# Multi-query attention: pacing value products and waiting VectorE work by ScalarE's clock

## The chip, the cores and the metric

The kernel runs on one core of a Trainium2 chip. A core has five engines that run side by side, each through its own list of instructions in a fixed order: TensorE (PE in the profile, its weight loads PEld) multiplies matrices, ScalarE (ACT) evaluates the exponential, VectorE (DVE) does elementwise work, GpSimd (POOL) and SyncE (SP) here mostly issue DMAs. The metric is device time in microseconds. The kernel before takes 1087.03 us, the median of six runs that lie between 1085.57 and 1087.64 us.

## The reference

```python
def setup_inputs():
    batch, seq_len, embed_dim = (8, 1024, 1024)
    num_heads = 16
    head_dim = embed_dim // num_heads
    # q: (8, 1024, 16, 64); k, v: (8, 1024, 64), float32

def reference(q, k, v):
    q = q.transpose(0, 2, 1, 3)
    k = k[:, None, :, :].copy()
    v = v[:, None, :, :].copy()
    scores = np.matmul(q, k.transpose(0, 1, 3, 2)) / np.sqrt(head_dim)
    weights = np.exp(scores - np.max(scores, axis=-1, keepdims=True))
    weights = weights / np.sum(weights, axis=-1, keepdims=True)
    attn_out = np.matmul(weights, v)
    return attn_out.transpose(0, 2, 1, 3).astype(np.float32)
```

Sixteen query heads of a batch share one key and one value head. The kernel leaves out the maximum, sums the exponentials with a matrix product by ones, and divides at the end.

## The kernel before, in words

The work is cut into 64 pairs (8 batches of 8 head pairs), and a pair `p` into 8 key tiles `j` of 128 keys. For a key tile TensorE makes two score tiles (`unit`, L134; tile `sc`, 128 x 2 x 512, three buffers in PSUM), one for each half of the queries. A score tile becomes weights in one of two ways. For most key tiles ScalarE takes the exponential (L147) straight into `wt`. For 71 of the 512 key tiles (9 of every 64, `is_dve`) VectorE makes it (`exp_dve`): two instructions `z` that take the two score tiles out of PSUM (L158, issued at once), and then six more, `f`, `t`, `g` (L170 to L174), `t`, `g` and `wt` (L176 to L178), which go on a list `late` and are issued when the planner finds room. Score tiles of such a key tile are woven with those of the next one, so ScalarE has its own tiles meanwhile.

The value products follow. `av_slot` makes slot `i` of a pair's 24: eight slots with ones (group 0, L193, the sums), eight for each half of the queries with the values (groups 1 and 2, L201). In each group the VectorE-made tile comes last. A group adds up in one accumulator `acc`, out of two PSUM buffers (`b1p`), and VectorE copies it to `ots` (L208). After group 2 a DMA transpose turns the result (`turn`), and `finish` puts the reciprocal (L223) and the normalising product (L230, then the output DMA) on `late`.

The order of the instructions is written out when the program is built (`manual_schedule`), by a loop over 512 cycles `cy`, one for each key tile: two score tiles, then value slots up to a quota, then waiting VectorE work. Three things set it. The quota is three slots a cycle, 12 cycles behind the scores (`LAG`). The list `late` is served while VectorE's planned time `busy` is below `(cy + 1) * T_CYCLE`, with planned costs per instruction (`T_TS`, `T_TT`, ...). And `av_slot` calls `force`, which issues whatever is left of a tile's six instructions just ahead of the first product that reads it. When the chip runs, each engine goes through its list in that order and waits where an operand or a buffer isn't ready; the planner's times play no part then. The pool of weight tiles has `LAG + 8` buffers.

Of the kernel before, what the change touches and what calls it, by code (L numbers as in the profile page):

```python
# [22 lines left out]
LAG = 12  # L23
T_CYCLE = 1.53
# [4 lines left out]
def kernel(  # L29
# [45 lines left out]
    otq: dict = {}  # L75
    late: list = []
# [22 lines left out]
    def trans_k(b):  # L99
        st = kst[b]  # L100
        kps = b1p.tile([P, S], FP16, tag="b1", name=f"kps{b}")
# [80 lines left out]
    def av_slot(p, i):  # L182
# [3 lines left out]
        if n == 0:  # L186
            acc[p] = b1p.tile([P, QC], FP32, tag="b1", name=f"acc{p}_{grp}")
# [17 lines left out]
        if n == NKT - 1:  # L205
            if grp == 0:
                ots[p] = otsp.tile([P, 3, QC], FP16, tag="ots", name=f"ots{p}")
            vec(T_COPY, lambda: nc.vector.tensor_copy(out=ots[p][:, grp, :], in_=a))  # L208

    def turn(p):  # L210
        otq[p] = otqp.tile([P, 13, P], FP16, tag="otq", name=f"otq{p}")[:, 0:12, :]
        nc.sync.dma_start_transpose(
            out=otq[p], in_=ots[p].rearrange("p g x -> p (g x)")
        )

    def finish(p, cycle):
        b, hp = divmod(p, HP)
        o = otq[p]
# [3 lines left out]
        def reciprocal():  # L222
            nc.vector.reciprocal(  # L223
# [5 lines left out]
        def normalise():  # L229
            nc.vector.tensor_tensor(  # L230
# [13 lines left out]
        late.append((None, cycle, T_NORM, normalise))  # L244

# [20 lines left out]
    slots = [(p, i) for p in range(NP) for i in range(3 * NKT)]  # L266

# [4 lines left out]
    with tc.manual_schedule(engines={ENG.PE, ENG.Activation, ENG.DVE}):  # L272
# [4 lines left out]
        cy = 0  # L277
        while cy < NCY or done < len(slots) or late:
            w, c = divmod(cy, NKT)
# [5 lines left out]
            busy[0] = max(busy[0], cy * T_CYCLE)  # L285
            if cy < NCY:
                for t, h in units[2 * cy : 2 * cy + 2]:
                    unit(t // NKT, NQC * (t % NKT) + h)
            quota = 3 * (cy + 1 - LAG) + max(0, cy + 1 - (NCY - 2 * NKT))
            if cy >= NCY:  # L290
                quota = len(slots)
            while done < min(quota, len(slots)):
                p, i = slots[done]
                if NKT * p + NKT - 1 >= cy and i % NKT + NKT * p >= cy:
# [3 lines left out]
                if i == 3 * NKT - 1:  # L298
                    turn(p)
                    finish(p, cy + 6)  # L300
            nb = w // HP + 1
            if nb < B and w % HP == HP - 2:
                if c == 2:
                    cast_k(nb)
                if c == 7:
                    trans_k(nb)
            while True:
                e = next((e for e in late if cy >= e[1] or done == len(slots)), None)
# [35 lines left out]
```

## Time and profile before

| | |
|---|---|
| median of six runs | 1087.03 us (1085.57 to 1087.64) |
| the profiled execution | 1086.96 us, of which the span from first to last instruction is 1085.2 us |
| TensorE's mean granted clock | 0.909 of full speed |
| PE busy | 813.0 us, 75% of the span |
| ACT busy | 825.7 us, 76% |
| DVE busy | 780.3 us, 72% |
| DMA | 89 GB/s over the span |

The rows are of one profiled execution. A busy time counts overlap of neighbouring instructions on an engine, so one activation of 1.02 us may stand 0.9 us after the one before. "Idle before" is the time in which an engine had nothing to do ahead of an instruction, with the instruction that ended it. No engine is busy throughout, and the chain of waits that ended last is spread over three of them: ACT 33%, DVE 29%, PE 28%.

### The profile page before, as it was taken

The numbers are of one execution on the slowest core, as the hardware profiler recorded it, in microseconds if no ns is written. First come the engines' busy times: TensorE is split into PE (matmuls) and PEld (weight loads), VectorE is DVE, ScalarE is ACT, GpSimd is POOL, SyncE is SP. The second block draws the span as 40 slices with busy tenths as digits, with TensorE's granted clock in tenths as the row PEclk, the third lists the DMA queues.
The fourth block names the chain that finished last, engine by engine and source line by source line (L and its number), as shares of the span: only waits on it lengthen the run. The fifth ranks groups of instructions, "written<-read, shape, count | busy, mean of one in ns | idle before, by whom it ended". The sixth has DMA issues, their size and how long they took to land.

```text
span 1085.2 us, 15328 instructions
## 1 busy us (share of the span) xinstructions
PE 813.0 (75%) x6208; PEld 234.6 (22%) x6208; DVE 780.3 (72%) x914; ACT 825.7 (76%) x883; POOL 64.1 (6%) x78
## 2 busy tenths in 40 slices
PE   3887778857788577876778777787777877788775
PEld 1222222212222122221222212222222222122121
DVE  1788677965779757796678956689567885678863
ACT  4998688956789477995779858797577976778763
POOL 3000000000000000000000000000000000000000
PEclk9999898987999789997899979899789998899888
DMA  9365465643656445573455635465354654434324
GB/s 135 54 108 107 73 103 88 108 82 66 101 88 104 87 73 95 85 127 66 76 96 91 114 73 90 76 100 105 63 98 71 108 95 73 88 64 88 78 49 107
DMA packets 317766, 96.41 MB, mean 89 GB/s; under 512 B 252160, under 2 KB 317696, under 8 KB 317696
## 3 DMA queue, kind: packets, MB, share of 16 engines
q1 hardware_dynamic: 242816, 77.62, 33.7%
q0 software_dynamic: 74880, 17.83, 17.6%
q8 instruction: 48, 0.79, 0.3%
q14 instruction: 22, 0.18, 0.1%
HBM read 37.75 MB, written 33.55 MB: 66 GB/s over the span
## 4 chain that ended last, share of the span: by engine, by line
ACT 33%; DVE 29%; PE 28%; issue 7%; DMA 2%; ACTq 0%; POOL 0%; DVEq 0%; POOLq 0%
DMA qt_126<-qn_104 1%; DMA qn_104<-in_q_dram 1%; PE acc_1_2671 L201 0%; DMA otq_10800<-ots_10762 0%; PE acc_1_6347 L201 0%; PE acc_1_6855 L201 0%; PE acc_1_8031 L201 0%; PE acc_1_4507 L201 0%; PE acc_1_9371 L201 0%; PE acc_1_2835 L201 0%; PE acc_1_5847 L201 0%; PE acc_1_9535 L201 0%; PE acc_1_1659 L201 0%; PE acc_1_9863 L201 0%; PE acc_1_3167 L201 0%
## 5 line engine op out<-in xcount | busy, mean ns | idle before, releaser
L193 PEld LDWEIGHTS <-ones_98 128*32 128x32 f16 x2048 | 42.5, 95 | 239.3 <-issue 224.6
L134 PEld LDWEIGHTS <-k2t_124 64*128 64x128 f16 x256 | 12.3, 97 | 65.7 <-issue 64.5
L134 PEld LDWEIGHTS <-k2t_1183 64*128 64x128 f16 x256 | 11.5, 95 | 49.1 <-issue 48.9
L134 PEld LDWEIGHTS <-k2t_6543 64*128 64x128 f16 x256 | 11.4, 95 | 48.8 <-issue 48.6
L134 PEld LDWEIGHTS <-k2t_2523 64*128 64x128 f16 x256 | 11.3, 95 | 49.3 <-issue 49.1
L134 PEld LDWEIGHTS <-k2t_7883 64*128 64x128 f16 x256 | 11.3, 95 | 48.5 <-issue 48.3
L134 PEld LDWEIGHTS <-k2t_3863 64*128 64x128 f16 x256 | 11.3, 95 | 48.7 <-issue 48.4
L134 PEld LDWEIGHTS <-k2t_5203 64*128 64x128 f16 x256 | 11.2, 96 | 48.3 <-issue 48.2
L134 PEld LDWEIGHTS <-k2t_9223 64*128 64x128 f16 x256 | 11.0, 95 | 46.4 <-issue 46.2
L201 PEld LDWEIGHTS <-v_351 128*64 128x64 f16 x256 | 12.1, 118 | 24.9 <-issue 21.8
L201 PEld LDWEIGHTS <-v_4363 128*64 128x64 f16 x256 | 12.1, 118 | 24.6 <-issue 21.4
L201 PEld LDWEIGHTS <-v_8383 128*64 128x64 f16 x256 | 12.3, 114 | 21.4 <-issue 16.1
L201 PEld LDWEIGHTS <-v_5703 128*64 128x64 f16 x256 | 11.9, 116 | 22.9 <-issue 19.5
L201 PEld LDWEIGHTS <-v_1683 128*64 128x64 f16 x256 | 11.8, 115 | 23.2 <-issue 19.7
L201 PEld LDWEIGHTS <-v_3023 128*64 128x64 f16 x256 | 11.8, 115 | 23.1 <-issue 19.7
L201 PEld LDWEIGHTS <-v_7043 128*64 128x64 f16 x256 | 11.8, 115 | 22.7 <-issue 19.4
L201 PEld LDWEIGHTS <-v_102 128*64 128x64 f16 x256 | 11.4, 112 | 20.2 <-issue 16.4
L158 DVE TENSOR_SCALAR z_4_174<-sc_8_170 128x1024 uint16<-128x1024 f32 x1 | 1.2, 1223 | 16.3 <-PE sc_8_170 L134 16.3
L147 ACT ACTIVATE wt_0_137<-sc_0_134 128x1024 f16<-128x1024 f32 x1 | 1.0, 1023 | 15.2 <-PE sc_0_134 L134 15.2
L134 PE MATMUL sc_0_134<-qt_126,k2t_124 64*128 64x512 f16 x2 | 0.6, 593 | 10.0 <-DMA qt_126<-qn_104 10.0
L147 ACT ACTIVATE wt_7_6522<-sc_14_6519 128x1024 f16<-128x1024 f32 x1 | 1.0, 1023 | 7.0 <-PE sc_14_6519 L134 7.0
L147 ACT ACTIVATE wt_7_5182<-sc_14_5179 128x1024 f16<-128x1024 f32 x1 | 1.0, 1023 | 7.0 <-PE sc_14_5179 L134 7.0
(4438 smaller groups left out, 2908.0 us busy)
## 6 DMA issues: line engine op xcount, KB each, us to landing
out_dram<-osb_423 SPq DMA_DIRECT2D x1, 512.0 KB, 3.9
out_dram<-osb_584 SPq DMA_DIRECT2D x1, 512.0 KB, 3.8
out_dram<-osb_751 SPq DMA_DIRECT2D x1, 512.0 KB, 4.8
out_dram<-osb_915 SPq DMA_DIRECT2D x1, 512.0 KB, 4.8
out_dram<-osb_1084 SPq DMA_DIRECT2D x1, 512.0 KB, 3.2
out_dram<-osb_1260 SPq DMA_DIRECT2D x1, 512.0 KB, 4.8
out_dram<-osb_1424 SPq DMA_DIRECT2D x1, 512.0 KB, 3.8
out_dram<-osb_1590 SPq DMA_DIRECT2D x1, 512.0 KB, 3.8
```

The source lines that it names most:

```text
L134: nc.tensor.matmul(sc[:, h, :], k2t[64 * h : 64 * h + 64, j * P : (j + 1) * P], qt[p].rearrange("p c x -> p (c x)")[64 * h : 64 * h + 64, ...
L147: nc.scalar.activation(out=wt[p, j][:, :, c * QC : (c + 1) * QC], in_=sc, func=EXP, scale=ascale)
L158: vec(2 * T_COPY, lambda: nc.vector.tensor_scalar(out=z[:, :, c * QC : (c + 1) * QC], in0=sc, scalar1=15 * ONE, scalar2=None, op0=ALU.add,))
L193: nc.tensor.matmul(a[32 * g : 32 * g + 32, :], ones16, w[:, h, cq * QC : (cq + 1) * QC], start=(n == 0), stop=(n == NKT - 1), tile_positio ...
L201: nc.tensor.matmul(a[64 * h : 64 * h + 64, :], vt[:, j, :], w[:, h, cq * QC : (cq + 1) * QC], start=(n == 0), stop=(n == NKT - 1), tile_po ...
```

## The change

Every instruction of the kernel before is there after it, and no other; each engine has as many rows as before. What changes is the order:

- The planner's time is now `clock`, which grows by `T_ACT` = 0.905 us for each score tile that ScalarE takes and by nothing for VectorE's; before it was 1.53 us for every cycle.
- The quota of value slots follows that clock: 24 slots in `t_pair`, the clock's advance over a mean pair, and `LAG` = 14 key tiles behind. Towards the end the quota is also raised by 4.5 slots a cycle. The pool of weight tiles grows from 20 to 22 buffers.
- Within a cycle waiting VectorE work now comes ahead of the value slots, and behind the score tiles.
- The copy of an accumulator is no longer issued at once: it goes on a list `first` for the next cycle, served ahead of `late`; `release` issues it at the latest when another tile of the two-buffer pool is taken. The DMA transpose follows the copy of group 2, and `finish` is due five cycles after that copy.
- The planner now also counts the two VectorE jobs of a new batch's keys.

```diff
--- before.py
+++ after.py
@@ -20,8 +20,8 @@
 GB = 0.07826797
 
 DVE_TILES = 9
-LAG = 12
-T_CYCLE = 1.53
+LAG = 14
+T_ACT = 0.905
 T_COPY, T_REC, T_NORM, T_TS, T_TT = 0.6, 0.2, 1.13, 0.6, 1.13
 
 
@@ -73,6 +73,8 @@
     acc: dict = {}
     ots: dict = {}
     otq: dict = {}
+    cy = [0]
+    first: list = []
     late: list = []
     busy = [0.0]
 
@@ -98,6 +100,7 @@
 
     def trans_k(b):
         st = kst[b]
+        release()
         kps = b1p.tile([P, S], FP16, tag="b1", name=f"kps{b}")
         for c in range(NKT):
             nc.tensor.transpose(
@@ -184,6 +187,7 @@
         j = sorted(range(NKT), key=lambda j: (is_dve(NKT * p + j), j))[n]
         force((p, j))
         if n == 0:
+            release()
             acc[p] = b1p.tile([P, QC], FP32, tag="b1", name=f"acc{p}_{grp}")
         a = acc[p]
         w = wt[p, j]
@@ -205,9 +209,16 @@
         if n == NKT - 1:
             if grp == 0:
                 ots[p] = otsp.tile([P, 3, QC], FP16, tag="ots", name=f"ots{p}")
-            vec(T_COPY, lambda: nc.vector.tensor_copy(out=ots[p][:, grp, :], in_=a))
+
+            def evacuate():
+                nc.vector.tensor_copy(out=ots[p][:, grp, :], in_=a)
+                if grp == 2:
+                    turn(p)
+
+            first.append((None, cy[0] + 1, T_COPY, evacuate))
 
     def turn(p):
+        finish(p, cy[0] + 5)
         otq[p] = otqp.tile([P, 13, P], FP16, tag="otq", name=f"otq{p}")[:, 0:12, :]
         nc.sync.dma_start_transpose(
             out=otq[p], in_=ots[p].rearrange("p g x -> p (g x)")
@@ -215,11 +226,11 @@
 
     def finish(p, cycle):
         b, hp = divmod(p, HP)
-        o = otq[p]
         osb = osbp.tile([P, NKT, 2 * D], FP32, tag="osb", name=f"osb{p}")
         rec = recp.tile([P, NQC, 4, 2], FP32, tag="rec", name=f"rec{p}")
 
         def reciprocal():
+            o = otq[p]
             nc.vector.reciprocal(
                 out=rec,
                 in_=o[:, 0:4, :].rearrange(
@@ -227,6 +238,7 @@
             )
 
         def normalise():
+            o = otq[p]
             nc.vector.tensor_tensor(
                 out=osb.rearrange("p i (h d) -> p (i h) d", h=2),
                 in0=o[:, 4:12, :].rearrange("p i (h d) -> p (i h) d", h=2),
@@ -242,6 +254,11 @@
 
         late.append((None, cycle, T_REC, reciprocal))
         late.append((None, cycle, T_NORM, normalise))
+
+    def release():
+        while first:
+            e = first.pop(0)
+            vec(e[2], e[3])
 
     NT = NP * NKT
 
@@ -264,6 +281,7 @@
             t += 1
     NCY = NT
     slots = [(p, i) for p in range(NP) for i in range(3 * NKT)]
+    t_pair = T_ACT * 2 * NKT * (1 - DVE_TILES / 64)
 
     load_kv(0)
     for p in range(3):
@@ -274,43 +292,41 @@
         trans_q(0)
         trans_q(1)
         done = 0
-        cy = 0
-        while cy < NCY or done < len(slots) or late:
-            w, c = divmod(cy, NKT)
+        clock = 0.0
+        while cy[0] < NCY or done < len(slots) or first or late:
+            w, c = divmod(cy[0], NKT)
             if c == 0:
                 load_q(w + 3)
                 trans_q(w + 2)
                 if w % HP == 2 and w // HP + 1 < B:
                     load_kv(w // HP + 1)
-            busy[0] = max(busy[0], cy * T_CYCLE)
-            if cy < NCY:
-                for t, h in units[2 * cy : 2 * cy + 2]:
-                    unit(t // NKT, NQC * (t % NKT) + h)
-            quota = 3 * (cy + 1 - LAG) + max(0, cy + 1 - (NCY - 2 * NKT))
-            if cy >= NCY:
+            busy[0] = max(busy[0], clock)
+            for t, h in units[2 * cy[0] : 2 * cy[0] + 2]:
+                unit(t // NKT, NQC * (t % NKT) + h)
+                clock += 0.0 if is_dve(t) else T_ACT
+            nb = w // HP + 1
+            if nb < B and w % HP == HP - 2:
+                if c == 2:
+                    vec(T_COPY * 2, lambda: cast_k(nb))
+                if c == 7:
+                    vec(T_COPY, lambda: trans_k(nb))
+            while True:
+                e = next((e for e in first + late if cy[0] >= e[1] or cy[0] > NCY), None)
+                if e is None or (cy[0] < NCY and busy[0] + e[2] / 2 > clock):
+                    break
+                (first if e in first else late).remove(e)
+                vec(e[2], e[3])
+            quota = 3 * NKT * (clock / t_pair - LAG / NKT)
+            quota = max(quota, 3 * NKT * (NP - 1) - 4.5 * (NCY - 1 - cy[0]))
+            if cy[0] >= NCY:
                 quota = len(slots)
             while done < min(quota, len(slots)):
                 p, i = slots[done]
-                if NKT * p + NKT - 1 >= cy and i % NKT + NKT * p >= cy:
+                if NKT * p + i % NKT + 1 > cy[0]:
                     break
                 av_slot(p, i)
                 done += 1
-                if i == 3 * NKT - 1:
-                    turn(p)
-                    finish(p, cy + 6)
-            nb = w // HP + 1
-            if nb < B and w % HP == HP - 2:
-                if c == 2:
-                    cast_k(nb)
-                if c == 7:
-                    trans_k(nb)
-            while True:
-                e = next((e for e in late if cy >= e[1] or done == len(slots)), None)
-                if e is None or (cy < NCY and busy[0] + e[2] / 2 > (cy + 1) * T_CYCLE):
-                    break
-                late.remove(e)
-                vec(e[2], e[3])
-            cy += 1
+            cy[0] += 1
 
 
 # ---- launch: one core; inputs and outputs as the reference has them ----
```

On VectorE, the end of the work on the VectorE-made tile 7 of the fourth batch's fifth pair. Names with `_7_` (`z`, `f`, `t`, `g`, `wt`) are that tile's steps; `z_6` belongs to the next such tile, `otq`, `rec` and `osb` to the output of an earlier pair. In the kernel before, the list there reads:

```order
L223 RECIPROCAL rec_4767<-otq_4764 128x16
L230 TENSOR_TENSOR osb_4766<-otq_4764,rec_4767 128x1024
L170 TENSOR_SCALAR f_7_4869<-z_7_4844 128x2048
L172 TENSOR_SCALAR t_7_4870<-f_7_4869 128x2048
L158 TENSOR_SCALAR z_6_4986<-sc_12_4982 128x2x512
L174 TENSOR_SCALAR g_7_4871<-f_7_4869 128x2048
L176 TENSOR_TENSOR t_7_4870<-f_7_4869,t_7_4870 128x2048
L177 TENSOR_TENSOR g_7_4871<-t_7_4870,g_7_4871 128x2048
L178 TENSOR_TENSOR wt_7_4843<-z_7_4844,g_7_4871 128x2048
L208 CAST ots_5005<-acc_0_4943 128x512
```

The tile's own `z` lie further up; the last step stands just ahead of the copy of the accumulator that adds the tile up. In the changed kernel, from the tile's own `z` on:

```order
L161 TENSOR_SCALAR z_7_4831<-sc_14_4827 128x2x512
L161 TENSOR_SCALAR z_7_4831<-sc_15_4854 128x2x512
L214 CAST ots_4865<-acc_0_4796 128x512
L234 RECIPROCAL rec_4793<-otq_4794 128x16
L242 TENSOR_TENSOR osb_4792<-otq_4794,rec_4793 128x1024
L173 TENSOR_SCALAR f_7_4858<-z_7_4831 128x2048
L214 CAST ots_4865<-acc_1_4867 128x512
L175 TENSOR_SCALAR t_7_4859<-f_7_4858 128x2048
L177 TENSOR_SCALAR g_7_4860<-f_7_4858 128x2048
L179 TENSOR_TENSOR t_7_4859<-f_7_4858,t_7_4859 128x2048
L180 TENSOR_TENSOR g_7_4860<-t_7_4859,g_7_4860 128x2048
L181 TENSOR_TENSOR wt_7_4830<-z_7_4831,g_7_4860 128x2048
```

The six steps, which ran past the next tile's `z`, now follow their `z` with a reciprocal, a normalising product and two copies between, and end before the next tile's `z`.

On VectorE, two pairs later, the copies of the accumulators (`ots<-acc_0`, `acc_1`, `acc_2` are groups 0, 1, 2). In the kernel before:

```order
L176 TENSOR_TENSOR t_5_5160<-f_5_5159,t_5_5160 128x2048
L177 TENSOR_TENSOR g_5_5161<-t_5_5160,g_5_5161 128x2048
L178 TENSOR_TENSOR wt_5_5131<-z_5_5132,g_5_5161 128x2048
L208 CAST ots_5349<-acc_0_5291 128x512
L208 CAST ots_5349<-acc_1_5351 128x512
L223 RECIPROCAL rec_5278<-otq_5275 128x16
L230 TENSOR_TENSOR osb_5277<-otq_5275,rec_5278 128x1024
L170 TENSOR_SCALAR f_4_5313<-z_4_5284 128x2048
L172 TENSOR_SCALAR t_4_5314<-f_4_5313 128x2048
```

The copies of groups 0 and 1 stand one behind the other, with 8 value slots of TensorE between their two accumulators. In the changed kernel, for the same pair:

```order
L214 CAST ots_5374<-acc_0_5315 128x512
L179 TENSOR_TENSOR t_4_5294<-f_4_5293,t_4_5294 128x2048
L180 TENSOR_TENSOR g_4_5295<-t_4_5294,g_4_5295 128x2048
L181 TENSOR_TENSOR wt_4_5273<-z_4_5274,g_4_5295 128x2048
L214 CAST ots_5374<-acc_1_5376 128x512
L234 RECIPROCAL rec_5311<-otq_5312 128x16
L161 TENSOR_SCALAR z_4_5438<-sc_8_5434 128x2x512
L161 TENSOR_SCALAR z_4_5438<-sc_9_5453 128x2x512
L214 CAST ots_5374<-acc_2_5415 128x512
L242 TENSOR_TENSOR osb_5310<-otq_5312,rec_5311 128x1024
```

The copy of group 1, which stood directly behind that of group 0, now has three steps of another tile ahead of it, and two `z` stand between it and the copy of group 2.

On TensorE, two cycles around a VectorE-made tile (score tiles `sc_10` and `sc_11` go to VectorE; repeats of a product and the weight loads are left out). In the kernel before:

```order
L134 MATMUL sc_10_5128<-qt_4693,k2t_3863 128x512
...
L134 MATMUL sc_12_5134<-qt_4693,k2t_3863 128x512
...
L193 MATMUL acc_0_5113<-wt_3_4916,ones_98 32x512
...
L193 MATMUL acc_0_5113<-wt_4_4937,ones_98 32x512
...
L193 MATMUL acc_0_5113<-wt_5_4962,ones_98 32x512
...
L134 MATMUL sc_13_5151<-qt_4693,k2t_3863 128x512
...
L134 MATMUL sc_11_5155<-qt_4693,k2t_3863 128x512
...
L193 MATMUL acc_0_5113<-wt_7_4991,ones_98 32x512
...
L193 MATMUL acc_0_5113<-wt_6_4985,ones_98 32x512
...
L201 MATMUL acc_1_5176<-wt_0_4849,v_3023 64x512
...
L134 MATMUL sc_14_5179<-qt_4693,k2t_3863 128x512
```

Three slots stand between each two score tiles and the next two. In the changed kernel:

```order
L137 MATMUL sc_10_5111<-qt_4687,k2t_3831 128x512
...
L137 MATMUL sc_12_5117<-qt_4687,k2t_3831 128x512
...
L205 MATMUL acc_2_5085<-wt_7_4830,v_3012 64x512
...
L197 MATMUL acc_0_5129<-wt_0_4836,ones_98 32x512
...
L137 MATMUL sc_13_5134<-qt_4687,k2t_3831 128x512
...
L137 MATMUL sc_11_5138<-qt_4687,k2t_3831 128x512
...
L197 MATMUL acc_0_5129<-wt_1_4873,ones_98 32x512
...
L197 MATMUL acc_0_5129<-wt_2_4888,ones_98 32x512
...
L137 MATMUL sc_14_5153<-qt_4687,k2t_3831 128x512
```

Two slots stand there now, and three or four in cycles whose score tiles both go to ScalarE.

## Rows read from the trace of the kernel before

**Rows 1.** The page, part 1: busy time (share of the span) and instructions of each engine

```profile
PE 813.0 (75%) x6208; PEld 234.6 (22%) x6208; DVE 780.3 (72%) x914; ACT 825.7 (76%) x883; POOL 64.1 (6%) x78
```

**Rows 2.** ScalarE in order of time, 485 to 495 us: start, duration, what, [idle before]

```profile
485.55 1.12 ACT L147 ACTIVATE wt_5_4962<-sc_11_4964 128x1024 f16<-128x1024 f32 x1
486.45 1.14 ACT L147 ACTIVATE wt_7_4991<-sc_14_4988 128x1024 f16<-128x1024 f32 x1
493.36 1.02 ACT L147 ACTIVATE wt_7_4991<-sc_15_5010 128x1024 f16<-128x1024 f32 x1 [5.77 <-PE sc_15_5010 L134]
```

**Rows 3.** TensorE in order of time, 486 to 495 us

```profile
486.13 0.40 PE L193 MATMUL acc_0_4943<-wt_0_4698,ones_98 128*32 128x512 f16 x4
491.59 0.62 PE L193 MATMUL acc_0_4943<-wt_7_4843,ones_98 128*32 128x512 f16 x4 [5.06 <-DVE wt_7_4843 L178]
...
492.71 0.61 PE L134 MATMUL sc_15_5010<-qt_4527,k2t_3863 64*128 64x512 f16 x2
...
493.67 0.64 PE L201 MATMUL acc_1_5007<-wt_2_4735,v_3023 128*64 128x512 f16 x2
494.10 0.64 PE L201 MATMUL acc_1_5007<-wt_3_4751,v_3023 128*64 128x512 f16 x2
```

**Rows 4.** VectorE in order of time, 483 to 493 us

```profile
483.25 0.25 DVE L223 RECIPROCAL rec_4767<-otq_4764 128x16 f32<-128x16 f16 x1
483.53 1.22 DVE L230 TENSOR_TENSOR osb_4766<-otq_4764,rec_4767 128x1024 f32<-128x1024 f16 x1
484.67 0.69 DVE L170 TENSOR_SCALAR f_7_4869<-z_7_4844 128x2048 uint16<-128x2048 uint16 x1
485.39 0.69 DVE L172 TENSOR_SCALAR t_7_4870<-f_7_4869 128x2048 f16<-128x2048 uint16 x1
486.00 1.22 DVE L158 TENSOR_SCALAR z_6_4986<-sc_12_4982 128x1024 uint16<-128x1024 f32 x1
487.13 0.68 DVE L174 TENSOR_SCALAR g_7_4871<-f_7_4869 128x2048 f16<-128x2048 uint16 x1
487.73 1.22 DVE L176 TENSOR_TENSOR t_7_4870<-f_7_4869,t_7_4870 128x2048 f16<-128x2048 uint16 x1
488.98 1.22 DVE L177 TENSOR_TENSOR g_7_4871<-t_7_4870,g_7_4871 128x2048 f16<-128x2048 f16 x1
490.31 1.23 DVE L178 TENSOR_TENSOR wt_7_4843<-z_7_4844,g_7_4871 128x2048 uint16<-128x2048 uint16 x1
492.25 0.69 DVE L208 CAST ots_5005<-acc_0_4943 128x512 f16<-128x512 f32 x1 [0.72 <-PE acc_0_4943 L193]
```

**Rows 5.** The waits of TensorE: us in total, times, longest

```profile
PE acc_0_6453 L193 <- DVE wt_6_6325 L178: 5.3, 1, 5.3
...
PE acc_0_9805 L193 <- DVE wt_3_9613 L178: 1.9, 1, 1.9
```

**Rows 6.** The waits of ScalarE

```profile
ACT wt_7_5182 L147 <- PE sc_14_5179 L134: 7.0, 1, 7.0
```

**Rows 7.** VectorE in order of time, one copy out of an accumulator

```profile
537.10 0.69 DVE L208 CAST ots_5349<-acc_1_5351 128x512 f16<-128x512 f32 x1 [5.07 <-PE acc_1_5351 L201]
```

**Rows 8.** Busy time by stretch: PE, PEld, DVE, ACT, POOL, granted clock, DMA

```profile
454.00:463.00 9.00, 7.81 (x72) 2.41 (x68) 7.81 (x10) 9.00 (x11) 0.00 (x0) 1.00 0.39 71
448.90:474.60 25.70, 22.85 (x188) 6.83 (x188) 21.00 (x25) 24.11 (x26) 1.75 (x2) 0.97 0.59 101
512.00:515.70 3.70, 3.70 (x24) 1.08 (x20) 0.69 (x1) 1.94 (x2) 0.00 (x0) 0.58 0.19 37
```

**Rows 9.** ScalarE in order of time, first and last activation

```profile
17.21 1.02 ACT L147 ACTIVATE wt_0_137<-sc_0_134 128x1024 f16<-128x1024 f32 x1 [15.20 <-PE sc_0_134 L134]
...
1068.18 1.10 ACT L147 ACTIVATE wt_7_10720<-sc_15_10722 128x1024 f16<-128x1024 f32 x1
```

**Rows 10.** DMA transposes of the output: issue to landing in us

```profile
otq_421<-ots_323 SPq DMA_TRANSPOSE x1, 3.6
...
otq_913<-ots_817 SPq DMA_TRANSPOSE x1, 6.7
```

## The prediction

> **What bounds the kernel now.** I read the page's busy times first, then ScalarE in order of time, then who waits for whom, and last TensorE and VectorE around one long wait.
>
> The busy times name no bound: three engines stand near 75% [rows 1]. But ScalarE's own pace is plain. While it has work it starts an activation every 0.90 to 0.91 us (486.45 less 485.55), and then it stands idle for 5.77 us [rows 2]. From its first activation at 17.21 us to its last at 1068.18 us are 1051.0 us [rows 9]; the 882 activations (883 instructions less one table load, rows 1) need 881 x 0.905 = 797.3 us of that. So 253.7 us, nearly a quarter of the span, is ScalarE without a score tile. That is all there is to win there.
>
> TensorE tells why a tile is missing. At 486.13 us it issues the last product that is ready, then waits 5.06 us for wt_7, made by VectorE, at the head of its list; the score tile that ScalarE wants (sc_15) stands two value slots behind, and starts at 492.71 us [rows 3]. The waits of this kind form one family: 45 of them in the list of waits, from 5.3 us down to 1.9 us [rows 5]. They add up to 158.8 us by my addition over that view, and ScalarE's waits behind them are longer, up to 7.0 us [rows 6], for two reasons. The score tile comes a slot or two after the product, and TensorE restarts at the lower level: right after the wait two slots start 0.43 us apart, against about half that in flow [rows 3]; a stretch behind such a wait shows a granted clock of 0.58, a stretch in flow 1.00 [rows 8], which are the levels 1.2 and 2.4 GHz, the first slightly averaged.
>
> And VectorE is late there not for want of time. The wt_7 chain was still at f at 484.67 us, with a reciprocal, a normalising product and another tile's z ahead of or between its steps [rows 4]. Elsewhere VectorE stands idle for a copy whose accumulator TensorE has not finished, 5.07 us in one place [rows 7], with waiting exponential steps behind that copy. Each engine waits in turn for the other.
>
> **The change, part by part.** Nothing is added or removed; all of it is order, so the sum is: fill + ScalarE's or VectorE's pace, whichever is longer + what is still lost + tail.
>
> The waits for wt. I count in the two orders from a tile's second z to its wt. Before, wt_7 has 15 instructions of VectorE behind its second z, up to and with wt: two copies, one z of the next tile, one reciprocal, one normalising product, six steps of its own and the last four of the tile before: by the distances of rows 4 and 0.61 to 0.69 us a copy, 1.3 + 1.13 + 0.28 + 1.14 + 5.74 + 4.41 = 14.0 us. Meanwhile ScalarE has 11 activations of its own, 10.0 us, until TensorE asks for wt_7. Short by 4.0 us, plus up to two activations by which TensorE runs ahead of ScalarE (three score buffers, one in use): at most 5.8 us, and 5.06 us was measured [rows 3]. After, the same tile has ten: two copies, 0.28 us, 1.14 us and its own six (0.72 + 0.61 + 0.60 + 1.25 + 1.33 + 1.23 = 5.74 us by rows 4), 8.4 us, against 14 activations, 12.7 us: 4.3 us to spare, 2.5 us with TensorE's lead. Over the repeating eight pairs the narrowest is tile 6, where the new batch's keys come between: 12.6 us against 16 activations, 14.5 us, so about level once the lead is off; tile 5 has 12.9 against 16.3 us, and the others 7.6 to 9.3 us against 18 to 24 us. So I take the 45 waits as gone but for about one microsecond in eight pairs.
>
> The copies. A copy now stands a cycle later, behind that cycle's z, so VectorE reaches it after the group is complete: waits as in rows 7 go. What it costs is the accumulator's buffer, held a cycle longer; the group after next needs it 8 slots later, over two cycles, which covers a copy of 0.69 us. If that cover failed, TensorE would wait about 1 us a group.
>
> The slots. In the two cycles of a VectorE-made tile ScalarE gets two score tiles, 1.81 us, and TensorE had four score tiles and six slots in them; in a stretch of 25.70 us with no wait for wt, 26 activations (23.5 us) ran [rows 8], 2.2 us lost around two to three such tiles, about 0.9 us each. Four slots instead of six take away two at some 0.22 us (half of 0.43), so I put 0.45 us for each. The slots not given there go to the other cycles, where TensorE has room: in 454 to 463 us it is busy 7.81 of 9.00 us with three a cycle while ScalarE runs without a gap [rows 8]. The bounds are nothing and the old 0.9 us.
>
> VectorE as the next bound. This is what is late next. Eight pairs have 9 tiles (18 z at 1.13 us = 20.3, nine chains at 5.74 = 51.7), 24 copies (at 0.61 to 0.69, 14.6 to 16.6), 8 reciprocals at 0.28 (2.2), 8 normalising products at 1.14 (9.1), and some 2 us of work on keys: 100 to 102 us, less up to 2.7 us where another instruction now fills the 0.1 us between dependent steps [distances in rows 4]. ScalarE has 110 activations, 99.6 us. The two are level at about 100 us for eight pairs, and VectorE can't be let idle. With 9 x 0.45 = 4 us lost I get 104 us.
>
> The reciprocal. It now comes five cycles after group 2's copy, and for half of the pairs only 4.1 to 5.7 us of VectorE work stand between. The transpose needs 3.6 us from issue to landing, at worst 6.7 us [rows 10]. With 3.6 us nothing is waited for; with 6.7 us up to 2.6 us. I take nothing for the likeliest and keep the rest as a rival.
>
> Lag and pools. The products start later, which is filled at the end by 4.5 slots a cycle (about 1 us of a cycle's 1.81, beside two score tiles); the last pair's 24 slots and the output stay behind the last activation as before. Fill and tail stay: 17.2 us, and 1085.2 - 1068.2 = 17.0 us [rows 9].
>
> Sum: 17.2 + 8 x 104 + 17.0 = 866 us of span; the profiled execution has 1.8 us outside its span (1086.96 against 1085.2), so 868 us. That execution lies 0.07 us below the median of the runs, so nothing is added. The floor, with ScalarE never idle, is 17.2 + 797.3 + 17.0 + 1.8 = 833 us; with 0.9 us lost for each of 71 tiles and one microsecond of wt wait in eight pairs it is 833 + 64 + 8 = 905 us. Near the floor I don't trust three engines at 88 to 100% in step, so the likeliest case's own range is 837 to 905 us.
>
> **The rivals.** *VectorE is the bound and waits for transposes.* For: it is level with ScalarE by the sum above, SP's list gives each transpose only its distance to the reciprocal, and a shorter span packs the same transfers closer. Against: most transposes land in about 3.6 us, and 16 us passed between issue and use before. Price: four of eight pairs at 2.0 us, and 102 us of work: 102 + 8 + 4 = 114 us for eight pairs, 17.2 + 912 + 17 + 1.8 = 948 us; half of it 908 us.
>
> *It doesn't do what it says: VectorE trails so far that TensorE still waits for wt.* For: the planned costs (z 1.2, steps 0.6 and 1.13) make 95 us for eight pairs where the rows make 100, so VectorE is later than planned. Against: ScalarE can't run further ahead of a late z than three score buffers, so the lag can't grow. If tiles 7, 6 and 5 kept waits that cost ScalarE 7.0 us [rows 6], eight pairs take 104 + 21 = 125 us, in all 1036 us.
>
> *TensorE never leaves the lower level: slower.* With the long waits gone, short ones stay in every cycle, for a score buffer. If these kept the clock at 1.2 GHz, a slot takes 0.43 us and a score tile about 0.4 to 0.5 us (492.71 us, and the following rows), so a pair takes 24 x 0.43 + 16 x 0.48 = 18.0 us, 64 pairs 1152 us, in all 1188 us. It decides as soon as TensorE's pair at the granted level exceeds ScalarE's 12.5 us. Against: in the flowing stretch just those short waits are there, and the clock is 1.00 [rows 8]. The Trainium skill, page "TensorE: Matmul & The Clock Gate", section "A second HAM failure mode: psum-queue depth-cycling", speaks for this rival: it tells of a kernel in which frequent short idle times between groups of products, from cycling PSUM buffers, made the clock swing between the levels. By that rule the time would lie towards 1188 us; the flowing stretch, at 1.00, goes against it.
>
> **How the numbers follow.** Likeliest case 80% (868 us), VectorE with transposes 11% (908 to 948), waits for wt remain 5% (1036), low clock 4% (1188, slower than before). The range goes from 837 us to 935 us, which takes in the lower half of the second case. A difference of 0.2%, 2.2 us, is about what runs of this kernel can tell from none. Faster: the first three, 0.955; within 0.2%: 0.005, no case ends there; slower: 0.04.
>
> **What would show it.** Right: the family "TensorE waits for wt from VectorE" is gone from the list of waits but for tile 6; ScalarE idles under 70 us between first and last activation; VectorE is over 88% busy and its waits for accumulators are under 1 us; the mean granted clock is above 0.95. Wrong: waits of VectorE for otq (second case), of TensorE for wt (third), TensorE for accumulator copies at 1 us a group (the cover of the copies), or a clock near 0.6 in flow. Were ScalarE's pitch no longer 0.905 us, the sum itself would fall.

## The result, and the profile after

The changed kernel takes 862.75 us (median of ten runs, 862.37 to 863.21) against 1086.91 us for the kernel before: a ratio of 0.794, 95% interval 0.7931 to 0.7944. The forecast was 868 us.

The profiled execution's span is 861.0 us. The page's busy times, as in [rows 1]:

```profile
PE 753.7 (88%) x6208; PEld 230.9 (27%) x6208; DVE 767.3 (89%) x914; ACT 815.7 (95%) x883; POOL 65.6 (8%) x78
```

ScalarE, which was busy for 76% of the span, is now at 95%; its busy time hardly moved (825.7 to 815.7 us), the span closed in around it. Eight pairs in the middle by stretch (columns as in [rows 8]):

```profile
400.00:503.50 103.50, 93.63 (x778) 28.63 (x776) 96.50 (x116) 101.62 (x111) 8.10 (x9) 1.00 0.70 116
```

In 103.5 us stand 111 activations, 100.5 us at ScalarE's pitch of 0.905 us from start to start; the granted clock is 1.00 and no engine is far from full. The first and last activation, as in [rows 9]:

```profile
17.49 1.02 ACT L150 ACTIVATE wt_0_137<-sc_0_134 128x1024 f16<-128x1024 f32 x1 [15.47 <-PE sc_0_134 L137]
...
845.57 1.07 ACT L150 ACTIVATE wt_7_10709<-sc_15_10711 128x1024 f16<-128x1024 f32 x1
```

They are 828.1 us apart, and 881 x 0.905 = 797.3 us of it is work: ScalarE idles 30.8 us where it idled 253.7 us, counted as all time beyond the pitch. The waits of TensorE for a VectorE-made tile, as in [rows 5], first and last of them:

```profile
PE acc_0_10606 L197 <- DVE wt_5_10462 L181: 0.4, 1, 0.4
...
PE acc_0_5129 L197 <- DVE wt_6_4973 L181: 0.3, 1, 0.3
```

There are eight, 2.5 us in all, where 45 added up to 158.8 us. Seven are at tile 6, once in eight pairs. VectorE in order of time, for the same tile as in [rows 4]:

```profile
391.04 1.23 DVE L161 TENSOR_SCALAR z_7_4831<-sc_15_4854 128x1024 uint16<-128x1024 f32 x1 [0.58 <-PE sc_15_4854 L137]
392.19 0.68 DVE L214 CAST ots_4865<-acc_0_4796 128x512 f16<-128x512 f32 x1
392.78 0.24 DVE L234 RECIPROCAL rec_4793<-otq_4794 128x16 f32<-128x16 f16 x1
393.06 1.23 DVE L242 TENSOR_TENSOR osb_4792<-otq_4794,rec_4793 128x1024 f32<-128x1024 f16 x1
394.20 0.69 DVE L173 TENSOR_SCALAR f_7_4858<-z_7_4831 128x2048 uint16<-128x2048 uint16 x1
394.96 0.69 DVE L214 CAST ots_4865<-acc_1_4867 128x512 f16<-128x512 f32 x1
...
396.76 1.22 DVE L179 TENSOR_TENSOR t_7_4859<-f_7_4858,t_7_4859 128x2048 f16<-128x2048 uint16 x1
398.02 1.22 DVE L180 TENSOR_TENSOR g_7_4860<-t_7_4859,g_7_4860 128x2048 f16<-128x2048 f16 x1
399.27 1.22 DVE L181 TENSOR_TENSOR wt_7_4830<-z_7_4831,g_7_4860 128x2048 uint16<-128x2048 uint16 x1
```

The second z starts at 391.04 us and wt ends at about 400.5 us. TensorE asks for that tile much later, and does not wait:

```profile
402.34 0.39 PE L137 MATMUL sc_13_4993<-qt_4522,k2t_3831 64*128 64x512 f16 x2 [0.53 <-ACT wt_7_4979 L150]
...
403.21 0.39 PE L137 MATMUL sc_0_5012<-qt_4687,k2t_3831 64*128 64x512 f16 x2
...
403.97 0.39 PE L197 MATMUL acc_0_4961<-wt_7_4830,ones_98 128*32 128x512 f16 x4
```

wt_7 is read at 403.97 us with no idle time before it. The one wait here is 0.53 us, for a score buffer that ScalarE holds, at the second score tile of VectorE's tile 6. ScalarE pays for it:

```profile
402.06 1.14 ACT L150 ACTIVATE wt_7_4979<-sc_15_4989 128x1024 f16<-128x1024 f32 x1
403.70 1.02 ACT L150 ACTIVATE wt_0_5015<-sc_0_5012 128x1024 f16<-128x1024 f32 x1 [0.50 <-PE sc_0_5012 L137]
```

The 1.64 us between these two starts are 0.73 us more than the pitch. VectorE had come late to this tile: its first score tile was complete at about 400.3 us, and the `z` that takes it out of PSUM started at 401.02 us, behind a copy:

```profile
400.42 0.68 DVE L214 CAST ots_4865<-acc_2_4918 128x512 f16<-128x512 f32 x1
401.02 1.21 DVE L161 TENSOR_SCALAR z_6_4974<-sc_12_4970 128x1024 uint16<-128x1024 f32 x1
```

Gaps like this, 0.1 to 0.74 us, are all that is left between first activation and last but for one of 1.1 us near the end. Of the 30.8 us, 26.6 us lie at this one place, the activation behind the second score tile of a VectorE-made tile, and they come in two sizes. At 29 of the 71 tiles TensorE waited more than 0.25 us ahead of that score tile, and ScalarE lost 0.67 us on average; at the other 42 it lost 0.17 us.

### The profile page after: what moved, and what is told of

It is laid out like the page before. It is cut to its first block, busy times and chain, and to the rows that moved or that the text cites. A ratio compares the mean times of both kernels' runs of the same rounds, so it can differ in the third digit from the quotient of the medians.

```text
span 861.0 us, 15286 instructions
## 1 busy us (share of the span) xinstructions
PE 753.7 (88%) x6208; PEld 230.9 (27%) x6208; DVE 767.3 (89%) x914; ACT 815.7 (95%) x883; POOL 65.6 (8%) x78
## 4 chain that ended last, share of the span: by engine, by line
ACT 57%; issue 16%; DVE 14%; PE 11%; DMA 2%; POOL 0%; ACTq 0%; POOLq 0%
DMA qt_126<-qn_104 1%; DMA qn_104<-in_q_dram 1%; DMA otq_10804<-ots_10764 0%; PE acc_1_10661 L205 0%; ACT wt_0_8856 L150 0%; ACT wt_5_759 L150 0%; ACT wt_5_594 L150 0%; ACT wt_5_10135 L150 0%; ACT wt_5_7459 L150 0%; ACT wt_5_6119 L150 0%; ACT wt_5_4779 L150 0%; ACT wt_5_2099 L150 0%; ACT wt_5_3439 L150 0%; ACT wt_5_8799 L150 0%; ACT wt_0_816 L150 0%
## 5 line engine op out<-in xcount | busy, mean ns | idle before, releaser
L197 PEld LDWEIGHTS <-ones_98 128*32 128x32 f16 x2048 | 40.7, 95 | 80.4 <-issue 64.3
L137 PEld LDWEIGHTS <-k2t_124 64*128 64x128 f16 x256 | 12.8, 96 | 63.9 <-issue 62.5
L137 PEld LDWEIGHTS <-k2t_7851 64*128 64x128 f16 x256 | 12.5, 93 | 48.8 <-issue 48.5
L137 PEld LDWEIGHTS <-k2t_5171 64*128 64x128 f16 x256 | 12.4, 93 | 48.5 <-issue 48.2
L137 PEld LDWEIGHTS <-k2t_6511 64*128 64x128 f16 x256 | 12.4, 93 | 48.5 <-issue 48.2
L137 PEld LDWEIGHTS <-k2t_3831 64*128 64x128 f16 x256 | 12.4, 93 | 48.5 <-issue 48.2
L137 PEld LDWEIGHTS <-k2t_2491 64*128 64x128 f16 x256 | 12.5, 93 | 48.3 <-issue 47.9
L137 PEld LDWEIGHTS <-k2t_1151 64*128 64x128 f16 x256 | 12.4, 93 | 48.4 <-issue 48.0
L137 PEld LDWEIGHTS <-k2t_9191 64*128 64x128 f16 x256 | 12.4, 93 | 47.2 <-issue 46.8
L161 DVE TENSOR_SCALAR z_4_174<-sc_8_170 128x1024 uint16<-128x1024 f32 x1 | 1.2, 1225 | 16.5 <-PE sc_8_170 L137 16.5
L205 PEld LDWEIGHTS <-v_8372 128*64 128x64 f16 x256 | 11.5, 109 | 16.5 <-issue 11.0
L150 ACT ACTIVATE wt_0_137<-sc_0_134 128x1024 f16<-128x1024 f32 x1 | 1.0, 1024 | 15.5 <-PE sc_0_134 L137 15.5
L205 PEld LDWEIGHTS <-v_102 128*64 128x64 f16 x256 | 10.7, 108 | 16.6 <-issue 12.9
L205 PEld LDWEIGHTS <-v_5692 128*64 128x64 f16 x256 | 10.7, 108 | 15.9 <-issue 12.2
L205 PEld LDWEIGHTS <-v_3012 128*64 128x64 f16 x256 | 10.7, 108 | 15.9 <-issue 12.2
L205 PEld LDWEIGHTS <-v_4352 128*64 128x64 f16 x256 | 10.7, 108 | 15.9 <-issue 12.2
L205 PEld LDWEIGHTS <-v_1672 128*64 128x64 f16 x256 | 10.7, 108 | 15.9 <-issue 12.2
L205 PEld LDWEIGHTS <-v_337 128*64 128x64 f16 x256 | 10.7, 108 | 15.9 <-issue 12.2
L205 PEld LDWEIGHTS <-v_7032 128*64 128x64 f16 x256 | 10.7, 108 | 15.9 <-issue 12.2
```

Source lines behind the costliest of these rows:

```text
L137: nc.tensor.matmul(sc[:, h, :], k2t[64 * h : 64 * h + 64, j * P : (j + 1) * P], qt[p].rearrange("p c x -> p (c x)")[64 * h : 64 * h + 64, ...
L150: nc.scalar.activation(out=wt[p, j][:, :, c * QC : (c + 1) * QC], in_=sc, func=EXP, scale=ascale)
L161: vec(2 * T_COPY, lambda: nc.vector.tensor_scalar(out=z[:, :, c * QC : (c + 1) * QC], in0=sc, scalar1=15 * ONE, scalar2=None, op0=ALU.add,))
L197: nc.tensor.matmul(a[32 * g : 32 * g + 32, :], ones16, w[:, h, cq * QC : (cq + 1) * QC], start=(n == 0), stop=(n == NKT - 1), tile_positio ...
L205: nc.tensor.matmul(a[64 * h : 64 * h + 64, :], vt[:, j, :], w[:, h, cq * QC : (cq + 1) * QC], start=(n == 0), stop=(n == NKT - 1), tile_po ...
```

## The experiments

Each run is timed beside the kernel before in the same session (1086.4 to 1086.7 us).

### The lag alone

```diff
 (kernel before)
-LAG = 12
+LAG = 14
```

> The kernel before with LAG = 14 (and so 22 weight buffers) and nothing else. Theory (pacing and order of VectorE's waiting work do most, the lag its part): counting VectorE instructions from a tile's second z to its wt against ScalarE activations until the first product that reads it, with 1.8 us of TensorE's lead, the kernel before is short by about 20 us in eight pairs (measured waits for wt 158.8 us in all); with lag 14 the same count is short by 63 us in all. At 1.2 us of ScalarE idle for each, and the slots' 0.9 us at each of 71 tiles still there, ScalarE idles some 140 us instead of 254: about 973 us. Rival (the lag alone is the gain): 865 to 885 us. Rival (the lag does nothing by itself): above 1060 us.

Measured: 993.69 us, ratio 0.915 (0.9132 to 0.9159). TensorE's waits for VectorE-made tiles (total us, times, longest):

```profile
PE acc L193 <- DVE wt L178: 76.3, 24, 5.2
```

Two cycles more room halve these waits (76.3 us; the count of instructions said 63). The lag alone gives 93 of the 224 us; the rival that it is the whole gain falls. The count was right in kind, 21 us too good in time.

### The changed kernel with the old lag

```diff
 (changed kernel)
-LAG = 14
+LAG = 12
```

> The changed kernel with LAG = 12 (20 buffers). Theory: the same count leaves TensorE short by 37 us in all over the kernel, at tiles 7, 6 and 5, so waits for wt come back in about three of eight pairs: 863 + 37 x 1.2 = about 907 us. Rival (order alone, lag irrelevant): 863 to 868 us. Rival (lag is all): above 1000 us.

Measured: 911.11 us, ratio 0.839 (0.8376 to 0.8401). The same wait:

```profile
PE acc L197 <- DVE wt L181: 35.8, 22, 2.4
```

35.8 us for a count of 37, and a time 4 us off: the room between a tile's z and its first product, counted in instructions, gives the waits.

### The copy at once

```diff
-            first.append((None, cy[0] + 1, T_COPY, evacuate))
+            vec(T_COPY, evacuate)
```

> The changed kernel with the accumulator copies issued at once, behind the group's last slot, instead of a cycle late. Theory (a copy that stands ahead of the next z makes VectorE wait for TensorE, as 204 us of waits over 148 copies did before): the chains have as much room as in the changed kernel, so no waits for wt by the count, but VectorE idles 0.5 to 1 us at each of 192 copies, 100 to 190 us, of which its idle 94 us cover a part: 900 to 950 us. Rival (the copies' place doesn't matter once the chains are on time): 863 to 870 us.

Measured: 866.47 us, ratio 0.798 (0.7961 to 0.7988). VectorE's waits for accumulators:

```profile
DVE ots L214 <- PE acc L205: 9.7, 14, 2.5
DVE ots L214 <- PE acc L197: 5.2, 9, 1.2
```

The theory falls: VectorE waits only 14.9 us at copies (14.1 us in the changed kernel), and 3.7 us of time are lost, as the rival said. With the rest of the order paced, the copy's own cycle hardly matters.

### The slots even again

```diff
-            quota = 3 * NKT * (clock / t_pair - LAG / NKT)
+            quota = 3 * (cy[0] + 1 - LAG)
```

> The changed kernel with the quota of value slots even again, three a cycle whatever ScalarE has in the cycle; VectorE's work is still paced by ScalarE's clock. Theory (two slots fewer at each VectorE-made tile save about 0.45 us): ScalarE's idle grows from 30 us to about 64 us, 895 us, with hardly any waits for wt. Rival (slots don't matter): 863 to 868 us.

Measured: 894.42 us, ratio 0.823 (0.822 to 0.8245), 32 us more than the changed kernel. The size is as forecast, but it isn't the slots' own time alone: waits for wt came back.

```profile
PE acc L197 <- DVE wt L181: 14.0, 9, 1.6
```

By ScalarE's rows, its idle time grew by 16.5 us at the activations behind a second score tile (26.6 to 43.1 us, 0.23 us a tile) and by 15.1 us elsewhere. So at most about half of the 32 us is what the two slots cost at the tile.

### VectorE's clock even again

```diff
-        clock = 0.0
+        clock = even = 0.0
...
-            busy[0] = max(busy[0], clock)
+            busy[0] = max(busy[0], even)
...
-                clock += 0.0 if is_dve(t) else T_ACT
+                clock += 0.0 if is_dve(t) else T_ACT
+                even += t_pair / (2 * NKT)
...
-                if e is None or (cy[0] < NCY and busy[0] + e[2] / 2 > clock):
+                if e is None or (cy[0] < NCY and busy[0] + e[2] / 2 > even):
```

> The changed kernel with VectorE's waiting work paced by an even clock (the same total, an equal advance in each cycle); the slots are still paced by ScalarE's clock. Theory: with the even clock a few more instructions stand between a tile's z and its wt (12.3 to 14.2 us instead of 7.6 to 12.9), short by 23 us in all with TensorE's lead, so 863 + 23 x 1.2 = about 890 us. Rival (the clock of the VectorE work does nothing): 863 to 868 us.

Measured: 881.34 us, ratio 0.811 (0.8098 to 0.8122); 19 us where 27 were expected, with more waits than counted (30.8 for 23 us):

```profile
PE acc L197 <- DVE wt L181: 30.8, 24, 2.7
```

ScalarE's idle time grew by 26.4 us elsewhere, but it fell by 7.8 us behind the second score tiles (26.6 to 18.8 us), which the forecast did not have.

### Waiting work behind the slots

The loop that serves `first` and `late` is moved behind the loop over value slots, and not changed.

```diff
-            while True:
-                e = next((e for e in first + late ...
             quota = ...
             while done < min(quota, len(slots)):
                 ...
+            while True:
+                e = next((e for e in first + late ...
```

> The changed kernel with the waiting VectorE work issued behind the value slots of a cycle, as before, instead of ahead. Theory: chains have the same room by the count (none short); copies stand at most one group of steps later; 863 to 872 us. Rival (this order carries the gain, through copies or forced chains): above 890 us.

Measured: 888.92 us, ratio 0.818 (0.8166 to 0.8192). A miss by 17 us: hardly any wait for wt (4.3 us), but VectorE waits for accumulators again:

```profile
DVE ots L214 <- PE acc L205: 41.8, 44, 4.0
...
DVE ots L214 <- PE acc L197: 13.9, 31, 1.2
```

55.7 us against 14.1 us in the changed kernel. Where a group ends and the next begins in one cycle, `release` issues the copy among that cycle's slots. With the waiting steps behind the slots, VectorE meets such a copy first and stands idle for TensorE with steps behind it that it could do; in the changed kernel those steps stand ahead of the copy. My count looked at chains alone and left this out. ScalarE's rows show where the time is lost: 24.0 of its 26.5 us of added idle time lie behind second score tiles (26.6 to 50.6 us). VectorE starts a tile's first z 1.22 us on average after its score tile is complete, against 0.42 us, and TensorE waits more than 0.25 us ahead of the second score tile at 67 of 71 tiles, against 29. The last stop of VectorE of over 0.15 us ahead of that z was at a copy for 60 of the 71 tiles, against 13. So the trace supports the copies as the cause of those 24 us, by way of a late z; no run takes them apart from the rest of the order.

### One tile fewer on VectorE

```diff
-DVE_TILES = 9
+DVE_TILES = 8
```

> The changed kernel with DVE_TILES = 8: one tile in eight pairs goes from VectorE to ScalarE. VectorE has some 8 us less in eight pairs, ScalarE two activations, 1.8 us, more (and 1/9 fewer places with 0.42 us of loss). Theory (ScalarE's pace bounds the changed kernel): 8 x 1.8 - 3 = 11 us slower, about 874 us. Rival (VectorE is the bound, as my sum had it level): faster, 845 to 858 us.

Measured: 859.52 us, ratio 0.791 (0.7895 to 0.7921). Faster, as only the rival allowed, but by 3 us, and 1.5 us above the rival's range. The page's busy times, and ScalarE's first and last stretch:

```profile
PE 752.0 (88%) x6208; PEld 225.0 (26%) x6208; DVE 715.4 (83%) x850; ACT 825.7 (96%) x899; POOL 64.2 (7%) x78
```

```profile
17.00 13.86 ACT L150 ACTIVATE wt<-sc 128x1024 f16<-128x1024 f32 x15 [14.98 <-PE sc L137]
...
829.63 13.90 ACT L150 ACTIVATE wt<-sc 128x1024 f16<-128x1024 f32 x15
```

The last activation starts at 829.63 + 14 x 0.905 = 842.3 us, so 898 activations span 825.3 us for 811.8 us of work: ScalarE has 14.5 us more work and idles 13.5 us instead of 30.8. VectorE now starts the first z 0.09 us on average after its score tile is complete, and no second score tile waits over 0.25 us. Whether this comes from VectorE's smaller load isn't shown by this run alone: it also puts every VectorE-made tile at place 4 of its pair, where the changed kernel lost only 0.13 us a tile already, against 0.11 us here.

### The normalising product twice

```diff
         def normalise():
             o = otq[p]
-            nc.vector.tensor_tensor(
+            for _ in range(2):
+                nc.vector.tensor_tensor(
...
```

> The changed kernel with the normalising product made twice (same result): 64 x 1.14 = 73 us more work for VectorE, unplanned. Theory (ScalarE bounds; VectorE has 94 us of idle time, but is level within a pair): about half shows, 880 to 905 us. Rival (VectorE is the bound): the whole 73 us shows, about 936 us. Rival (VectorE has true slack): 863 to 868 us.

Measured: 900.89 us, ratio 0.829 (0.8275 to 0.8299). Just over half of the 73 us shows, as expected. Now TensorE also waits for VectorE's z, which hold score buffers, and for wt (6.7 us). Most of the loss is again behind second score tiles, where ScalarE's idle time grew from 26.6 to 54.5 us:

```profile
PE 762.2 (85%) x6208; PEld 235.3 (26%) x6208; DVE 838.3 (93%) x978; ACT 819.7 (91%) x883; POOL 63.9 (7%) x78
```

```profile
PE sc L137 <- DVE z L161: 8.1, 17, 1.0
```

### Both clocks even and the work behind the slots

The edits of three experiments above together (the clock is one for both, `clock += t_pair / (2 * NKT)`).

> The changed kernel with both clocks even and the waiting VectorE work behind the slots: of the change only lag 14, the later copies and the counted key work are left. Undone singly these parts cost 31.7 us (slots), 18.6 us (VectorE's clock) and 26.2 us (order). Rival (the parts add up): 863 + 76 = about 939 us. Theory (they all feed one thing, the wt chains, and fail together): by the count the chains are 13.6 to 16.6 us long as in the kernel before with lag 14, short by 72 us in all, so waits for wt of 70 to 80 us and 985 to 1000 us, as that one's 993.7 us.

Measured: 992.69 us, ratio 0.913 (0.9117 to 0.9148). The parts do not add up to 939 us; they fail together:

```profile
PE acc L197 <- DVE wt L181: 85.1, 24, 4.7
```

85.1 us of waits, and the time of the kernel before with lag 14 (993.69 us). VectorE's waits at copies are back as well, although the copies are still issued a cycle late:

```profile
DVE ots L214 <- PE acc L205: 110.2, 57, 5.4
...
DVE ots L214 <- PE acc L197: 27.7, 38, 1.5
```

137.9 us: what makes VectorE wait at a copy is a late TensorE, more than the copy's cycle. So the later copy and the counted key work give nothing beside the lag alone, and what the change gains beyond the lag comes from the two clocks and the order together.

### Eight tiles and the normalising product twice

> The changed kernel with eight VectorE-made tiles in eight pairs and the normalising product made twice: VectorE has about as much work as in the changed kernel (one tile of 8 us less in eight pairs, 9.1 us more), ScalarE two activations more. The first kernel with eight tiles takes 859.5 us. Theory (what cost the changed kernel its last 30 us is VectorE being level with ScalarE): 872 to 885 us. Rival (it was where in the pair the VectorE-made tile falls; with eight tiles it is always tile 4): 859 to 864 us.

Measured: 893.23 us, ratio 0.822 (0.8208 to 0.8233): 34 us more than with the product once, and 8 us above the forecast. The tile's place is the same, so the rival, in which the place is all of it, falls.

```profile
PE 754.5 (85%) x6208; PEld 229.5 (26%) x6208; DVE 788.5 (88%) x914; ACT 831.0 (93%) x899; POOL 64.1 (7%) x78
```

```profile
17.10 13.86 ACT L150 ACTIVATE wt<-sc 128x1024 f16<-128x1024 f32 x15 [15.08 <-PE sc L137]
...
856.06 18.44 ACT L150 ACTIVATE wt<-sc 128x1024 f16<-128x1024 f32 x20 [0.99 <-PE sc L137]
```

The last activation starts at 856.06 + 19 x 0.905 = 873.3 us: 44.4 us idle instead of 13.5, with VectorE at 88% of the span. No product waits for wt here.

The trace doesn't bear out the theory's reason either, that VectorE is level with ScalarE. In one of the pairs, VectorE, then TensorE, then ScalarE:

```profile
408.32 0.69 DVE L214 CAST ots<-acc 128x512 f16<-128x512 f32 x1 [0.78 <-PE acc L205]
408.93 0.24 DVE L234 RECIPROCAL rec<-otq 128x16 f32<-128x16 f16 x1
409.21 2.48 DVE L243 TENSOR_TENSOR osb<-otq,rec 128x1024 f32<-128x1024 f16 x2
411.61 1.22 DVE L161 TENSOR_SCALAR z<-sc 128x1024 uint16<-128x1024 f32 x1
...
412.62 0.39 PE L137 MATMUL sc<-qt,k2t 64*128 64x512 f16 x2 [0.52 <-ACT wt L150]
...
413.93 2.85 ACT L150 ACTIVATE wt<-sc 128x1024 f16<-128x1024 f32 x3 [0.44 <-PE sc L137]
```

In 60 of 63 pairs the doubled product stands directly ahead of the first z, which then starts 1.15 us on average after its score tile is complete. At 60 tiles TensorE waits 0.52 us ahead of the second score tile and ScalarE loses 0.73 us, 43.8 us in all. In the pair shown VectorE has stood idle for 0.78 us at a copy just before. What counts here is what stands ahead of z in VectorE's list, and not only how full VectorE is.

### Eight tiles and the old lag

```diff
-DVE_TILES = 9
-LAG = 14
+DVE_TILES = 8
+LAG = 12
```

> The changed kernel with eight VectorE-made tiles and LAG = 12. With the tile always at place 4 the count leaves 14.5 us for a chain of 8.2 to 9.1 us, none short even at lag 12. Theory (the lag matters only through the room of the wt chains): 858 to 862 us, as with lag 14, and no wait for wt, though the same step cost the nine-tile kernel 48 us. Rival (a shorter lag costs by itself): above 870 us.

Measured: 862.37 us, ratio 0.794 (0.7922 to 0.7949). TensorE's waits hold no row for wt; the largest, and one that is new:

```profile
PE sc L137 <- ACT wt L150: 65.3, 217, 0.4
...
PE kps L106 <- DVE ots L214: 2.3, 7, 0.3
```

2.9 us more than with lag 14, just above the range given, against 48 us in the nine-tile kernel. The lag is worth what the room of the chains is worth, and the 2.9 us besides stay unexplained.

### Seventeen tiles in sixteen pairs

```diff
-    return t < NT - NKT and (t + 4) * DVE_TILES // 64 != (t + 3) * DVE_TILES // 64
+    return t < NT - NKT and (t + 4) * 17 // 128 != (t + 3) * 17 // 128
```

(and `DVE_TILES = 8.5`, which sets `t_pair`.)

> The changed kernel with 17 VectorE-made tiles in 16 pairs, between eight and nine in eight. ScalarE has one activation in eight pairs more than with nine tiles and one fewer than with eight; no chain is short by the count. If the loss at a tile follows how level VectorE is: 852 to 857 us, a minimum between the two. If it follows the tile's place in the pair (which wanders again): 859 to 863 us.

Measured: 859.55 us, ratio 0.791 (0.7897 to 0.7921). ScalarE's first and last stretch:

```profile
17.24 13.86 ACT L150 ACTIVATE wt<-sc 128x1024 f16<-128x1024 f32 x15 [15.22 <-PE sc L137]
...
829.81 12.97 ACT L150 ACTIVATE wt<-sc 128x1024 f16<-128x1024 f32 x14
```

The last activation starts at 829.81 + 13 x 0.905 = 841.6 us; 890 activations are 889 x 0.905 = 804.5 us of 824.3, so 19.8 us idle. With 9, 8.5 and 8 tiles in eight pairs ScalarE idles 30.8, 19.8 and 13.5 us, and its work is 797, 805 and 812 us: what VectorE is spared ScalarE has to do, and the time is flat at the minimum. My forecast of a dip fails, and 859.55 us lies in the range that I gave for the tile's place. Neither reason alone fits all runs. VectorE starts the first z 0.42, 0.24 and 0.09 us late on average with 9, 8.5 and 8 tiles, and the second score tile waits over 0.25 us at 29, 9 and no tiles. Both these kernels beat the changed one by 3 us (ratios 0.7908 and 0.7909 against 0.7938, intervals apart); no other run beats them.

## Why the prediction was right

**The bound and its cause.** ScalarE without score tiles was the loss, and its idle time fell by 222.9 us (253.7 to 30.8) where the time fell by 224 us. The chain behind it, TensorE waiting in order for wt, is what ended: 158.8 us to 2.5 us, and where experiments bring these waits back (76.3, 85.1, 35.8, 30.8 us) time comes back with them (131, 130, 48 and 19 us). These waits aren't the only loss: with the work behind the slots 26 us came back with 4.3 us of them. Counting a chain's instructions against ScalarE's activations gave these waits to about a quarter in four of the five experiments with more than 10 us of them (63, 72, 37 and 23 us counted); it missed the fifth, the even slots, with next to none counted and 14.0 us measured. The narrowest place was tile 6, as forecast, at 0.3 us rather than one.

**The sum.** Fill 17.5 us (17.2 forecast), first to last activation 828.1 us (832), tail 861.0 - 845.6 = 15.4 us (17.0), outside the span 1.8 us: 862.8 us. For its size the tail was the worst of the terms. I had carried it over, and the last pair's normalising product now starts about 10 us behind the start of the last activation instead of 11 us.

**Slots at a VectorE-made tile.** 0.45 us each was forecast, 30.8/71 = 0.43 us was measured. But I took it as the same at each tile and gave it to TensorE's slots alone. It is a mean of 0.67 us at 29 tiles and 0.17 us at 42 (and 4.2 us elsewhere), and making the slots even costs 0.23 us a tile by itself. With eight tiles the loss is 13.5 us over 63 tiles, 0.21 us each, half of it (6.8 us) behind second score tiles. So the agreement of the mean is in part luck: what I left out is how late VectorE comes to a tile's first z.

**Copies.** That waits of VectorE as in [rows 7] would go was right (206 us before, of which the list that I added up holds 204, and 14.1 us after). That the copy's later cycle does it was wrong: issued at once, it costs 3.7 us, and late copies in an unpaced order leave 137.9 us of these waits. The sign that none would reach 1 us held up to the last three pairs; near the end there are five of 1.0 to 2.5 us.

**VectorE level with ScalarE.** By busy time it was: 89% where over 88% was forecast, and 73 us more work cost 38 us (900.89 less 862.75). The sum put no loss on it, and it wasn't free. The loss at a VectorE-made tile goes with how late VectorE comes to the first z: 0.09 us late on average with eight tiles, 0.42 us in the changed kernel, 1.15 us with eight tiles and the product twice, for 0.11, 0.38 and 0.70 us lost at a tile. How much of that is VectorE's load and how much the place of the work ahead of z stays open, and so does why the second score tile then waits for ScalarE's buffer. The rival in which it waits for transposes did not come about. The list of waits has one row for them, at the very end, beside the longest wait at a copy:

```profile
DVE ots_10659 L214 <- PE acc_1_10661 L205: 2.5, 1, 2.5
DVE rec_10803 L234 <- DMA otq_10804<-ots_10764: 2.3, 1, 2.3
```

The same wait, 2.4 us, ended the kernel before. The transposes took 3.6 to 7.6 us from issue to landing, against 3.6 to 6.7 us. The margin of the reciprocal was thin but held: it started at least 0.4 us after the landing in every pair but the last.

**The lag.** My text priced it at nothing apart from the chains. That was right in kind, as the eight-tile kernels show, but it hid the largest single part of the gain: 93 of 224 us by itself, 48 us if undone last. The parts undone one at a time cost 48 + 32 + 26 + 19 + 4 = 129 us; the rest is theirs only together. The counted key work and the raised quota at the end were not undone one at a time.

**The low clock.** The mean granted clock is 0.995, as forecast above 0.95, although TensorE still waits up to half a microsecond for score buffers in many cycles. The Trainium skill, page "TensorE: Matmul & The Clock Gate", section "A second HAM failure mode: psum-queue depth-cycling", tells of a kernel in which short idle times made the clock swing. That does not show here: 103.5 us with such waits ran at 1.00. Where waits of up to 5 us remain (the lag alone, clock 0.941), the clock is lower.

## What to carry to other kernels

Where several engines run through fixed lists, an engine at 72% can be the one that is late: count, for each result, the work that stands ahead of it on its engine against the time until the first reader's place comes up, in units of the engine that should set the pace. Issue waiting work by that engine's clock and ahead of anything in the list that can itself wait, and leave a lead larger than the longest chain. Count also what stands ahead of an instruction that frees a scarce buffer, here the z. When the stalls are gone, shift work between the two engines that are level; here the minimum is flat.

## What was not expected of the hardware

ScalarE's pitch of 0.905 us is the same at 76% and at 96% busy, beside a DMA load that rose from 89 to 112 GB/s. And the short waits of TensorE, 0.2 to 0.5 us in many cycles, leave the granted clock at 1.00.
